# Two fill tiles and another order of the constant tiles in a one-layer hybrid encoder kernel

## The chip, the core and the metric

One NeuronCore of a Trainium2 chip runs the whole layer. The metric is the device time of one execution in microseconds (us); lower is better. The engines are called PE (TensorE, the matrix multiplier; PEld is its loading of stationary operands), DVE (VectorE), ACT (ScalarE), POOL (GpSimd) and SP (SyncE, which here only issues DMAs). SBUF is the on-chip memory from which PE reads both operands; each of its 128 partitions holds the same byte addresses, and "offset" below always means a tile's start address in a partition modulo 256 bytes.

## The reference

One encoder layer on x (1024 positions x 1024 features, float32):

```
h = rmsnorm(x);  p = h @ w_in                        (1024 x 3104)
yA = gb * dwconv3(gc * gv)                            gated short convolution
yB = silu(go) * headnorm(GLA_forward + GLA_backward)  gated linear attention, 4 heads, chunks of 64
x = x + rmsnorm(concat(yA, yB) @ w_out)
h = rmsnorm(x)
x = x + rmsnorm((silu(dwconv3(h @ w_up)_gate) * dwconv3(h @ w_up)_value) @ w_down)   D_FF = 2816
```

## The kernel before

Each large product is computed as three PE passes. An operand is split into a high part `h` (rounded to the fp32r format by an ACT copy, L687) and a low part `l` (the remainder, by a DVE subtraction, L688); then h x h, h x l and l x h are accumulated in PSUM. One PE instruction of these passes streams a moving operand of 128 partitions x 512 elements (2048 bytes per partition) through a stationary operand of 128 x 128 (512 bytes per partition), which a load instruction on PEld brings in first. In the trace's tile names the moving operand stands first behind the arrow and the stationary one second: `pa<-b1h,ug7h` streams b1h through ug7h into pa.

The stages, in order of time:

- The value projection (L345, streams of 272 elements) and the other input projections with the linear attention between them (`feature_chunk`, L232; L215 to L217 for the last one). The moving operands are hT (pool actp), the stationary ones weight pieces (pool wpool).
- `w_out_tile` (L734): eight row blocks of the output projection, 48 matmuls each. The moving operands are pieces of w_out, which lie where room is (pools mp, w2p, cvp); the stationary ones are the mixer's outputs yh, yl (actp). Between the blocks stand transposes (L762). At the end of the stage DVE makes the operands T1 to T5 of the next one.
- The up projection (`up(c)`, 22 units, L804). Each unit makes seven products of 12 matmuls, by a fast scheme that replaces eight block products by seven. The moving operands are b1, T1, T2 (actp) and T3, T4, T5 (pool act2, allocated from the right end of SBUF, behind pool mp's place). The stationary ones are weight pieces from `w_tile`, which takes six of every ten from wpool and four from w2p. While a unit runs, SP loads the next unit's weights, ACT and DVE split them, and DVE also adds the products into place and computes the convolutions (L961 to L963) and the gate (L1041, L1044).
- The down projection (`big_product`, `passes`, L1110): seven products over eleven pairs of feed-forward chunks. For each pair `operands(m, q)` loads both operands from HBM (SP, L1083 to L1088) and splits them; both parts of both operands lie in one tile of actp or act2, or (product 2, its first four pairs) in `w_tile` pieces.
- A last normalisation and the stores.

The POOL queue runs a side stream (`side`, `up_begin` to `down_end`, L93 to L130): it loads pieces of w_up and w_down, makes sums that the two fast schemes need, and stores them to HBM (tensors wud and wdd), from where SP loads them later. From unit 3 of the up projection on, each unit's first DVE addition (L988) releases an ACT copy `pace` (L991), for which one such job waits (two at units 8, 11 and 14). Three more jobs follow behind the up projection without a pace.

Where tiles lie: pools are placed one behind the other in the order in which they are opened. From the left: four small constants (to byte 1152), then cpool (ident, eps, prm), actp, ypool, wpool, rawp, `small`, and then the pools of the stages (gp, later w2p, cvp, sp and others). From the right end downwards: mp, later act2. A tile takes its size rounded up to 32 bytes. In cpool, ident (512 bytes, an identity matrix for transposes), eps (4) and prm (596) are allocated at L150, L152 and L276.

Of the kernel before, what the change touches and what calls it, by code (L numbers as in the profile page):

```python
# [8 lines left out]
F32 = mybir.dt.float32  # L9
# [7 lines left out]
P = 128  # L17
# [24 lines left out]
def kernel(  # L42
# [25 lines left out]
    w_up = w_up[0].rearrange("(k p) n -> p k n", p=P)  # L68
    w_down = w_down[0]

    cpool = ctx.enter_context(tc.tile_pool(name="cpool", bufs=1))
    actp = ctx.enter_context(tc.tile_pool(name="actp", bufs=4))
    ypool = ctx.enter_context(tc.tile_pool(name="ypool", bufs=8))
# [65 lines left out]
    def side(tile=row_tile, after=None, ahead=0):  # L139
# [5 lines left out]
        while len(begun) > ahead:  # L145
            end, i, t = begun.pop(0)
            with tc.issue_after(loads[-1].ins) if ahead else ExitStack():
                end(i, *t)

    ident = cpool.tile([P, P], F32, tag="ident", name="ident")  # L150
    make_identity(nc, ident)
    eps = cpool.tile([P, 1], F32, tag="eps", name="eps")  # L152
    nc.vector.memset(eps, EPS)
    small = ctx.enter_context(tc.tile_pool(name="small", bufs=4))

    pinned = [False]

# [45 lines left out]
    def act_table(name):  # L203
        tc.keep_in_program_order(nc.scalar.preload_act_table_set(name))
# [67 lines left out]
        yT[4 + h] = ypool.tile([P, L], F32, tag="y", name=f"yT{4 + h}")  # L272
        nc.scalar.activation(yT[4 + h], ps, AF.Silu)

    NPB = 21
    prm = cpool.tile([P, P + NPB], F32, tag="prm", name="prm")  # L276
    act_table("natural_log_exp_and_others")
    with ExitStack() as n1:
        np_ = n1.enter_context(tc.tile_pool(name="np", bufs=2))
# [131 lines left out]
        nc.tensor.transpose(pp[:, 0:P], stk[:, 0, :], ident)  # L411
        nc.tensor.transpose(pp[:, P : P + NPB], stk[0:NPB, 1, :], ident[0:NPB, 0:NPB])
        nc.vector.tensor_copy(prm, pp[:, 0 : P + NPB])

# [233 lines left out]
    def conv_steps():  # L648
        for j in range(4):
            yield from conv_tile(j, j == 3)  # L650
            yield

    fill = conv_steps()
# [582 lines left out]
```

## Time and profile before

| | |
|---|---|
| median of 3 runs | 1075.53 us (1074.16 to 1076.70) |
| the profiled execution | 1075.13 us, of which the span of its instructions is 1073.2 us |
| PE busy | 1057.0 us (98% of the span) |
| DVE busy | 801.8 us (75%) |
| ACT, POOL busy | 466.0 us (43%), 345.2 us (32%) |
| granted PE clock, mean | 0.999 of full |
| mean DMA rate | 196 GB/s |

A busy share sums an engine's instructions. PE's instructions overlap each other, so a PE that is busy all the time can still run faster or slower: its rate is the distance between the starts of two matmuls, which is read here from the chain of waits (the work that ended last, followed back from the end, with the stretch that each piece took). In the rows `xN` is a number of instructions, and L734 is line 734 of the program.

### The profile page before, as it was taken

The numbers are of one execution on the slowest core, as the hardware profiler recorded it, in microseconds if no ns is written. First come the engines' busy times: TensorE is split into PE (matmuls) and PEld (weight loads), VectorE is DVE, ScalarE is ACT, GpSimd is POOL, SyncE is SP. The second block draws the span as 40 slices with busy tenths as digits, with TensorE's granted clock in tenths as the row PEclk, the third lists the DMA queues.
The fourth block names the chain that finished last, engine by engine and source line by source line (L and its number), as shares of the span: only waits on it lengthen the run. The fifth ranks groups of instructions, "written<-read, shape, count | busy, mean of one in ns | idle before, by whom it ended". The sixth has DMA issues, their size and how long they took to land.

```text
span 1073.2 us, 14378 instructions
## 1 busy us (share of the span) xinstructions
PE 1057.0 (98%) x5409; PEld 871.0 (81%) x5409; DVE 801.8 (75%) x992; ACT 466.0 (43%) x654; POOL 345.2 (32%) x360
## 2 busy tenths in 40 slices
PE   8999999999999999999999999999999999999997
PEld 7998887888888888888888888888888777888886
DVE  6951369879867557988977988978998967556566
ACT  6431354463435234554344344343443435254452
POOL 2789500000000000004565564555546546400000
PEclk9999999999999999999999999999999999999999
DMA  8787511110255222167777877766976788976755
GB/s 287 271 273 257 177 41 40 40 40 21 72 164 168 79 79 95 44 195 245 258 239 244 280 251 229 249 211 180 298 262 223 264 323 294 351 244 229 243 176 216
DMA packets 163511, 210.64 MB, mean 196 GB/s; under 512 B 18273, under 2 KB 113650, under 8 KB 163442
## 3 DMA queue, kind: packets, MB, share of 16 engines
q1 hardware_dynamic: 142578, 134.48, 39.5%
q0 software_dynamic: 20288, 73.41, 19.5%
q10 hardware_dynamic: 576, 1.84, 0.4%
q8 instruction: 42, 0.69, 0.3%
q14 instruction: 27, 0.22, 0.1%
HBM read 146.52 MB, written 63.18 MB: 195 GB/s over the span
## 4 chain that ended last, share of the span: by engine, by line
PE 83%; DVE 8%; DMA 3%; ACT 2%; issue 2%; SPq 0%; DVEq 0%; ACTq 0%
PE pb L804 17%; PE pc L804 11%; PE pa L804 9%; PE pw L734 8%; PE pdb L1110 8%; PE pgc L232 4%; PE pgo L232 4%; PE pv L345 4%; PE pgv L232 3%; PE pqk L232 3%; PE pdd L1110 3%; PE pdc L1110 3%; PE pgb L232 2%; DVE d L688 1%; PE pdl L1110 1%
## 5 line engine op out<-in xcount | busy, mean ns | idle before, releaser
L100 POOL COPY wu10g<-pace 128x1 f32<-128x1 f32 x1 | 0.4, 354 | 365.7 <-ACT pace L991 365.7
L1110 PE MATMUL pdb<-d 128*128 128x512 f32 (+1 forms) x495 | 110.8, 384 | 0.4 <-DVE d L688 0.3
L1110 PEld LDWEIGHTS pdb<-d 128*128 128x128 f32 x495 | 90.5, 188 | 20.3 <-DVE d L688 1.6
L804 PE MATMUL pb<-t,uv 128*128 128x512 f32 x264 | 65.2, 396 | 0.0
L804 PEld LDWEIGHTS pb<-t,uv 128*128 128x128 f32 x264 | 49.6, 188 | 11.9
L988 DVE TENSOR_TENSOR cg<-cv,pb 128x512 f32<-128x512 f32 x22 | 15.1, 686 | 36.8 <-PE pb L804 16.6
L1041 ACT ACTIVATE uu<-uu 128x1024 f32<-128x1024 f32 x22 | 23.4, 1062 | 35.2 <-DVE uu L963 35.1
L1161 POOL DMA_DIRECT2D x2r<-x2d x4 | 2.1, 536 | 107.8 <-DMA d_8r<-actd 98.2
L1044 DVE TENSOR_TENSOR uu<-uu,uv 128x1024 f32<-128x1024 f32 x22 | 32.4, 1475 | 0.0
L962 DVE SCALAR_TENSOR_TENSOR uu<-cg,prm,uu 128x1023 f32<-128x1023 f32 x22 | 29.0, 1316 | 1.9
L1110 PE MATMUL pdc<-d 128*128 128x512 f32 x132 | 30.2, 390 | 0.0
L1110 PE MATMUL pdd<-d 128*128 128x512 f32 x132 | 30.2, 390 | 0.0
L963 DVE SCALAR_TENSOR_TENSOR uv<-cv,prm,uv 128x1023 f32<-128x1023 f32 x22 | 29.6, 1343 | 0.0
L873 ACT COPY cv<-pa 128x512 f32<-128x512 f32 x22 | 12.8, 587 | 38.1 <-PE pa L804 36.1
L963 DVE SCALAR_TENSOR_TENSOR uu<-cg,prm,uu 128x1023 f32<-128x1023 f32 x22 | 29.3, 1333 | 0.0
L1110 PEld LDWEIGHTS pdd<-d 128*128 128x128 f32 x132 | 24.8, 188 | 5.3
L1110 PEld LDWEIGHTS pdc<-d 128*128 128x128 f32 x132 | 24.8, 188 | 5.3
L962 DVE SCALAR_TENSOR_TENSOR uv<-cv,prm,uv 128x1023 f32<-128x1023 f32 x22 | 28.7, 1302 | 0.0
L570 DVE SCALAR_TENSOR_TENSOR S<-S,dec 64x128 f32<-64x128 f32 x56 | 19.2, 344 | 10.7 <-ACT S L561 8.5
L961 ACT ACTIVATE uv<-cv,prm 128x1024 f32<-128x1024 f32 x22 | 25.4, 1154 | 3.7 <-DVE cv L1021 3.5
L961 ACT ACTIVATE uu<-cg,prm 128x1024 f32<-128x1024 f32 x22 | 25.3, 1149 | 0.3 <-ACT d L687 0.3
L1018 DVE TENSOR_TENSOR cg<-cg,pc 128x512 f32<-128x512 f32 x22 | 15.0, 680 | 8.9 <-PE pc L804 8.9
(1314 smaller groups left out, 3252.3 us busy)
## 6 DMA issues: line engine op xcount, KB each, us to landing
actd<-as SPq DMA_DIRECT2D x20, 512.0 KB
x<-in_x_dram SPq DMA_DIRECT2D x16, 512.0 KB, 5.7
actd<-uu SPq DMA_DIRECT2D x10, 512.0 KB, 3.8
x2d<-x SPq DMA_DIRECT2D x8, 512.0 KB, 3.1
actd<-uu SPq DMA_DIRECT2D x10, 256.0 KB, 3.7
x2r<-x2d POOLq DMA_DIRECT2D x4, 512.0 KB, 5.5
x2r<-x2d SPq DMA_DIRECT2D x4, 512.0 KB, 4.5
out_dram<-o POOLq DMA_DIRECT2D x4, 512.0 KB, 7.1
```

The source lines that it names most:

```text
L232: nc.tensor.matmul(o[hf], wt[:, k, :], act[hf][a][:, k, :], start=(k == 0 and wt is wh and a == 0), stop=(k == KT - 1 and wt is wl))
L345: keep(nc.tensor.matmul(ps[:, n * 512 : n * 512 + VH], a[:, k, sl], w[:, k % 2, n * VH : (n + 1) * VH], start=(j == 0), stop=(j == 3 * KT ...
L570: nc.vector.scalar_tensor_tensor(S[0:DK, c + 1, :], S[0:DK, c, :], dec[0:DK, c : c + 1], S[0:DK, c + 1, :], op0=ALU.mult, op1=ALU.add)
L734: ins = nc.tensor.matmul(ps[:, n * HALF : (n + 1) * HALF], a[:, k, sl], w[:, n * HALF : (n + 1) * HALF], start=(i == 0 and q == 0), stop=( ...
L804: nc.tensor.matmul(o, w[:, k, :], m[:, k, :], start=start and k == 0 and q == 0, stop=k == 3 and q == 2, skip_group_check=True)
L961: nc.scalar.activation(u, src, AF.Copy, scale=ffn_tap(1, r))
L962: nc.vector.scalar_tensor_tensor(u[:, 1:L], src[:, 0 : L - 1], ffn_tap(0, r), u[:, 1:L], op0=ALU.mult, op1=ALU.add)
L963: nc.vector.scalar_tensor_tensor(u[:, 0 : L - 1], src[:, 1:L], ffn_tap(2, r), u[:, 0 : L - 1], op0=ALU.mult, op1=ALU.add)
L988: nc.vector.tensor_add(cg[:, hi], cv[:, lo], pb)
L1041: last_act[0] = nc.scalar.activation(ug, ug, AF.Silu)
L1044: nc.vector.tensor_mul(ug, ug, uv)
L1110: nc.tensor.matmul(o, a[:, 0, sl], b[:, 1, r], start=start and i == 0, stop=stop and i == 2, skip_group_check=True)
```

## The change

```diff
+    edge = ctx.enter_context(tc.tile_pool(name="edge", bufs=1, side="right"))
+    edge.tile([P, 56], F32, tag="fill", name="fill_r")
     cpool = ctx.enter_context(tc.tile_pool(name="cpool", bufs=1))
...
+    NPB = 21
+    eps = cpool.tile([P, 1], F32, tag="eps", name="eps")
+    prm = cpool.tile([P, P + NPB], F32, tag="prm", name="prm")
     ident = cpool.tile([P, P], F32, tag="ident", name="ident")
     make_identity(nc, ident)
-    eps = cpool.tile([P, 1], F32, tag="eps", name="eps")
     nc.vector.memset(eps, EPS)
     small = ctx.enter_context(tc.tile_pool(name="small", bufs=4))
+    small.tile([P, 48], F32, tag="fill", name="fill_l", bufs=1)
...
-    NPB = 21
-    prm = cpool.tile([P, P + NPB], F32, tag="prm", name="prm")
```

A fill of 224 bytes stands at the right end of SBUF, ahead of mp and act2; another of 192 bytes stands in `small`, ahead of all that follows it from the left; and ident comes behind eps and prm. No instruction reads or writes the fills. On every engine the same instructions stand in the same order as before, with the same waits; only addresses differ. Offsets (start address modulo 256) before and after, from the addresses in the built programs:

| tiles | bytes from the partition's start, before | offset before | after |
|---|---|---|---|
| actp, ypool, wpool, rawp (hT, yh, b1, T1, T2, most weight pieces, part of the down operands) | 2304 to 139776 | 0 | 0 |
| ident | 1152 | 128 | 0 |
| gp, w2p, cvp, sp (four of ten weight pieces, part of w_out, raw loads) | 142144 to about 180000 | 64 | 0 |
| mp, act2 (most of w_out, T3, T4, T5, part of the down operands) | 180192 to 229344 | 224 | 0 |

In unit 7 of the up projection the pieces ug7 and us7 lie in wpool and uv7 in w2p; its products follow each other as b1 x ug7, T2 x us7, b1 x ug7, T3 x us7, T1 x us7, T4 x uv7, T5 x us7 (moving x stationary).

The 128x512 matmuls by the offsets of their operands (moving / stationary) in the program before; after the change all of them are 0 / 0:

| line | 0/0 | 224/224, 64/64 | 224/0 | 0/64 | 224/64 | 64/0 | sum |
|---|---|---|---|---|---|---|---|
| L232, L215 to L217 | 960 | | | | | | 960 |
| L734 | | | 288 | | | 96 | 384 |
| L804 | 652 | | 472 | 404 | 320 | | 1848 |
| L1110 | 490 | 385 | | 8 | | 8 | 891 |

(L488 has eight more at 64/64.) The value projection's streams of 272 elements start at 0, 64, 128 and 192 before and after, since its halves are 1088 bytes long.

## Rows read from the trace of the kernel before

**Rows 1.** Page, part 1 and 2: busy us, share, instructions; granted clock in 40 slices.
```profile
PE   1057.0 (98%) x5409; PEld 871.0 (81%) x5409; DVE 801.8 (75%) x992; ACT 466.0 (43%) x654; POOL 345.2 (32%) x360
PEclk9999999999999999999999999999999999999999
```

**Rows 2.** Busy us (instructions) by stretch, then granted clock, DMA share, GB/s.
```profile
325.00:420.00 95.00, 95.00 (x437) 77.65 (x436) 55.81 (x101) 35.99 (x76) 0.00 (x0) 1.00 0.30 103
420.00:442.00 22.00, 21.89 (x104) 17.65 (x103) 21.89 (x40) 15.86 (x31) 0.00 (x0) 1.00 0.23 73
442.00:837.00 395.00, 395.00 (x1704) 319.78 (x1704) 341.54 (x342) 167.58 (x206) 195.26 (x193) 1.00 0.73 235
837.00:912.00 75.00, 73.08 (x313) 58.03 (x312) 56.80 (x45) 34.39 (x39) 43.03 (x41) 1.00 0.82 289
912.00:1073.20 161.20, 153.75 (x704) 127.61 (x704) 99.02 (x131) 68.95 (x104) 16.36 (x20) 0.99 0.71 243
```

**Rows 3.** PE lines: duration of one, ns min/median/max; first and last start.
```profile
L232 PE MATMUL pgo<-hTh,go2h x16: 389/389/389, 89.3 to 99.0; 128*128 128x512 f32 x16
...
L734 PE MATMUL pw<-wo6h,yl x16: 395/396/396, 329.3 to 411.9; 128*128 128x512 f32 x16
...
L1110 PE MATMUL pdc<-d x132: 387/389/398, 914.9 to 944.7; 128*128 128x512 f32 x132
```

**Rows 4.** Chain of waits: start us, us that the piece took, engine, output, line, matmuls.
```profile
313.96 0.87 PE pot L618 x8
...
325.74 55.73 PE pw L734 x240
381.47 1.75 PE tx L762 x16
```

**Rows 5.** The same chain: unit 7 of the up projection, and a product of the down projection.
```profile
558.84 2.76 PE pa L804 x12
561.60 2.72 PE pb L804 x12
564.32 2.72 PE pa L804 x12
567.04 2.80 PE pb L804 x12
569.84 2.74 PE pc L804 x12
572.59 2.81 PE pb L804 x12
575.40 2.80 PE pc L804 x12
...
945.12 30.09 PE pdb L1110 x132
```

**Rows 6.** The same chain between the up and the down projection.
```profile
837.10 0.70 DVE cg L988
...
857.94 6.45 DMA d_7r<-in_w_down_dram
...
874.18 11.35 DMA d_2r<-in_w_down_dram
...
892.28 8.61 DMA d_0r<-in_w_down_dram
...
903.98 4.84 DMA d_6r<-in_w_down_dram
...
912.23 2.80 PE pdb L1110 x11
```

**Rows 7.** POOL in order of time: start, us, instruction; in brackets what it waited for.
```profile
584.88 0.94 POOL L100 COPY wu15g<-pace 128x1 f32<-128x1 f32 x1 [2.28 <-ACT pace L991]
...
663.34 0.31 POOL L100 COPY wu19v<-pace 128x1 f32<-128x1 f32 x1 [2.81 <-DMA wud<-wu18g]
```

**Rows 8.** DVE groups in 130 to 190 us: count, busy us, mean ns, idle before.
```profile
L511 DVE TENSOR_TENSOR qd<-qd,m 128x1024 f32<-128x1024 f32 x2 | 2.5, 1225 | 1.6 <-ACT m L507 1.6
...
L191 DVE TENSOR_TENSOR qk2l<-qk2r,qk2h 128x1024 fp32r<-128x1024 f32 x1 | 1.2, 1224 | 3.2 <-ACT qk2h L190 3.2
```

## The prediction

> **What bounds the kernel now.** I read the page's busy shares first: PE has 98% of the span, DVE 75%, and the granted clock is at its full level, 2.4 GHz, in every slice [rows 1]. So only two things can bring time: PE's few waits, or the distance between its matmuls. The stretches say where each counts [rows 2]. From 325 to 420 (output projection) and from 442 to 837 us (up projection) PE is busy for the whole of the stretch and every other engine less; there the stage lasts as long as its matmuls stand apart. From 420 to 442 DVE is busy for 21.89 of 22.00 us: it makes T1 to T5, and a faster PE gains nothing. From 837 to 912 PE is busy for 73.08 of 75, yet the chain of waits does not run over it: it runs through DVE, the issue of operand loads and the loads themselves, 6.45, 11.35, 8.61 and 4.84 us of them [rows 6]. PE is nearly filled there, but its end is set by loads.
>
> Then the distances. The chain gives the time of whole products. In unit 7 of the up projection, seven products of 12 matmuls, one after the other on a PE that waits for nothing, take 2.76, 2.72, 2.72, 2.80, 2.74, 2.81 and 2.80 us [rows 5]. The four short ones are those whose operands both start at offset 0 (b1 and T2 or T1 with wpool pieces); the three long ones pair 224 with 0 or with 64. Short: 10.94 us / 48 = 227.9 ns per matmul. Long: 8.41 / 36 = 233.6 ns. The difference, 5.7 ns, stands inside one stage and one unit, beside the same DVE, POOL and DMA work. The output projection, where every moving operand starts at 224 or 64 and every stationary one at 0, takes 55.73 us / 240 = 232.2 ns [rows 4]. A product of the down projection, whose two operands mostly lie in one tile (0/0 or 224/224), takes 30.09 / 132 = 228.0 ns [rows 5]. So a tile at 224 is not slow in itself; two operands at different offsets are. The durations of single matmuls say the same: 389 ns in the input projections at 0/0 and in the down projection, 395 to 396 in the output projection [rows 3].
>
> **The change part by part.** It adds no instruction and takes none away; order and waits on every engine, SP's and POOL's queues among them, stay as they are. It moves addresses, and after it every 128x512 matmul is 0/0.
>
> - Output projection: 384 matmuls. (232.2 - 228.0) x 384 = 1.6 us. Its end starts the DVE work of 420 to 442, which keeps its length but starts earlier, so all 1.6 us pass through.
> - Up projection, 442 to 837: 395.00 us / 1704 = 231.8 ns now [rows 2]; at 227.9 the stretch is 3.9 x 1704 = 6.6 us shorter. (The other way: 1196 of 1848 matmuls have unequal offsets, x 5.7 ns = 6.8 us for all 22 units.) It passes through if DVE keeps up: 341.54 us of work against 395.00 now and 388.4 then, 88% busy. I count it whole.
> - 837 to 912: the chain of loads begins at DVE's addition at 837.10, right behind a product of PE, so it starts earlier by what came before and keeps its 75.1 us [rows 6]. PE's own gain here, some 70 pairs, I cost at nothing: the loads cover it.
> - Behind 912: nearly all pairs are equal already; the borders between actp and act2 tiles and the sixteen 0/64 and 64/0 matmuls are some 40 pairs x 6 ns = 0.2 us.
> - Input projections: all 0/0 already, nothing. Streams of 128: eight transposes with operands at 128 and 224 take 0.87 us and sixteen at 128 and 0 take 1.75 [rows 4], 109 ns each both times, so moving ident and the small operands costs or brings nothing.
> - DVE: a subtraction with all operands at 0 takes 1224 ns and a product with all at 224 takes 1225 [rows 8]; nothing.
> - The fills are never touched: nothing.
>
> Sum: 1.6 + 6.6 + 0.2 = 8.4 us. Against the profiled execution, 1075.13 - 8.4 = 1066.7; the median shown, 1075.53, lies 0.4 higher, so **1067.1 us**. What the trace doesn't show is how near an all-equal stage comes to its best product. Bounds: every matmul as in the shortest products, 2.72 / 12 = 226.7 ns, gives (231.8 - 226.7) x 1704 = 8.7, (232.2 - 226.7) x 384 = 2.1 and 1.3 x 528 = 0.7 in the down projection, together 11.5 us (1064.0); the other end is no gain. I take 227.9 to 228.0, because it is what equal pairs reach on average beside the same traffic, in two stages.
>
> Against the change speaks the Trainium skill, "TensorE: Matmul & The Clock Gate", sections "Back-to-back issue gap" and "Step-by-step: what each phase is for": the gap depends on the number of columns and the clock alone, and loading the next weights doesn't take read bandwidth from the running matmul. By it the sum would be 0 and the time 1075.5. The trace disagrees so far: 227.9 and 233.6 ns for the same columns at the same clock [rows 5].
>
> **The rivals.**
>
> *Offsets are not the cause.* What the slow products share could also be that one operand lies in the upper part of SBUF (above 142144 bytes) and the other in the lower. Then nothing changes: 1075.5 us. For it: 224/224 pairs lie in one tile and are fast. Against it: T4 with uv7 lie both in the upper part, at 224 and 64, and that product is the longest of the unit, 2.81 us [rows 5]. Chance 0.09.
>
> *Part is given back to the side stream.* From unit 8 on POOL's jobs no longer wait for `pace` (a job at 584.88 still does) but for their own stores (one at 663.34) [rows 7], so POOL runs at its own rate. By 585 PE has gained 1.6 + 6.6 x 143 / 395 = 4.0 us, by 837 8.2: POOL lags by 4.2 us more against PE, and its loads and stores then share the 16 DMA engines with the operand loads, which decide from 837 on. If those lose what POOL lags, 4.2 us go back: 1071.3. Against it: only the share of the loads that meets POOL's moves. It shows as longer waits of PE for d. Chance 0.17.
>
> *Slower.* The same place, one step worse. Of the four loads on the chain two took 11.35 and 8.61 us and two 6.45 and 4.84 [rows 6]. If PE's earlier arrival lets POOL's bursts meet the two short ones as well, at 11.35 each, that is 4.9 + 6.5 = 11.4 us more, against 8.4 gained: 1075.5 + 3.0 = 1078.5. It turns into a loss from 8.4 us of longer loads. Against it: POOL's traffic doesn't grow, and what it does later leaves room earlier. Chance 0.05.
>
> **How the numbers follow.** Forecast 0.69, the rivals 0.09, 0.17 and 0.05. A measurement of this kernel tells about 0.2%, 2.2 us, from no change. Forecast and partial give-back lie below 1073.4: 0.86, less 0.02 for a give-back that takes nearly all, 0.84 faster; same 0.11; slower 0.05. The range goes from the best-product bound, 1064.0, to 1072.0, just past the give-back, and leaves out the other two rivals and the tails, together under 0.2.
>
> **What would show it.** Right: unit 7's seven products all at 2.72 to 2.76 us; the 240-matmul piece of the output projection near 54.7 us in place of 55.73; 442 to 837 shrunk to some 388 us for the same matmuls; the 30.09 us products of the down projection unchanged; the stretch from the last up products to PE's piece at 912 still about 75 us. Wrong: products still at 2.80, which means the first rival; or products at 2.73 and that stretch grown by several us with PE waiting for d, which means the second or the third. A granted clock below full in any stage but the last would upset the sum too.

## The result, and the profile after

The changed kernel takes 1065.25 us, median of 4 runs (1063.65 to 1065.81), against 1075.07 us for the kernel before, median of 4 (1074.16 to 1076.70). The ratio is 0.9905, with a 95% interval of 0.9887 to 0.9922: 9.8 us faster. The forecast was 1067.1, in a range of 1064.0 to 1072.0. The profiled execution of the changed kernel took 1065.09 us, its span 1063.1 us, 10.1 less than before.

The diff adds lines near the top and takes two out further down, so most of the program stands four lines lower: L804 is now L808, L734 is L738, L1110 is L1114, L687 and L688 are L691 and L692, and so on.

The page of the changed kernel, which answers to [rows 1]:

```profile
PE 1045.8 (98%) x5409; PEld 871.3 (82%) x5409; DVE 800.1 (75%) x992; ACT 466.3 (44%) x654; POOL 344.0 (32%) x360
PEclk9999999999999999999999999999999999999999
```

There is the same number of instructions on every engine, and the granted clock is the same. PE's busy time fell by 11.2 us at an unchanged share.

The stretches, asked for at the same times as [rows 2] (busy us and instructions of PE, PEld, DVE, ACT, POOL; clock; DMA share; GB/s):

```profile
420.00:442.00 22.00, 21.84 (x104) 17.57 (x103) 21.98 (x40) 15.91 (x30) 0.00 (x0) 1.00 0.19 63
442.00:837.00 395.00, 394.56 (x1739) 325.76 (x1738) 348.00 (x346) 172.52 (x210) 199.45 (x197) 1.00 0.73 240
837.00:912.00 75.00, 71.97 (x313) 58.04 (x312) 53.57 (x42) 31.06 (x35) 45.38 (x42) 1.00 0.89 311
```

In 395 us PE now gets through 1739 matmuls, where it was 1704. DVE is busy for 348.00 of the 395 and just keeps up.

PE's groups by line (duration of one in ns, min/median/max; first and last start). The T4 and T5 products with uv, before the change:

```profile
L804 PE MATMUL pb<-t,uv x264: 391/396/400, 453.3 to 847.7; 128*128 128x512 f32 x132
```

The changed kernel; the second and third row answer to [rows 3]:

```profile
L808 PE MATMUL pb<-t,uv x264: 387/389/398, 450.8 to 837.6; 128*128 128x512 f32 x132
L738 PE MATMUL pw<-wo6h,yl x16: 389/389/389, 329.0 to 409.9; 128*128 128x512 f32 x16
L1114 PE MATMUL pdc<-d x132: 389/389/389, 904.9 to 934.5; 128*128 128x512 f32 x132
L1114 PE MATMUL pdl<-d x66: 279/336/389, 1024.5 to 1054.8; 128*128 128x512 f32 x33, 128*128 128x256 f32 x33
```

The first and last starts tell where the time went. The first matmul of T4 and T5 with uv starts 2.5 us earlier, the last one 10.1 us earlier. The down projection's pdc product, behind the stretch that loads decide, starts 10.0 us earlier (914.9 in [rows 3]). The last matmul starts 10.9 us earlier (1065.7 before).

The chain of waits, in the output projection and in unit 7 of the up projection; its pieces answer to [rows 4] and [rows 5]:

```profile
325.55 54.40 PE pw L738 x240
379.95 1.75 PE tx L766 x16
...
553.90 2.72 PE pa L808 x12
556.62 2.72 PE pb L808 x12
559.34 2.72 PE pa L808 x12
562.06 2.72 PE pb L808 x12
564.78 2.72 PE pc L808 x12
567.50 2.72 PE pb L808 x12
570.22 2.72 PE pc L808 x12
```

All seven products of the unit take 2.72 us, 226.7 ns per matmul. The 240 matmuls of the output projection take 54.40 us, also 226.7 ns each. Products of 128 columns are unchanged (1.75 for sixteen).

Behind the up projection the chain now stays with the loads and with ACT and DVE, which split what was loaded, to the end. Some of its pieces, which answer to [rows 6]:

```profile
827.23 0.70 DVE cg L992
...
848.14 5.95 DMA d_7r<-in_w_down_dram
...
865.75 10.73 DMA d_3r<-in_w_down_dram
...
906.21 5.41 DMA d_5r<-in_w_down_dram
...
923.96 7.06 DMA d_0r<-wdd
```

PE nevertheless hardly waits there; these are its waits of more than 0.3 us behind 442 us (which instruction waited for which: us in total, times, longest):

```profile
PE pdb L1114 <- DVE d L692: 1.2, 1, 1.2
PE pda L1114 <- DVE d_2l L692: 1.0, 1, 1.0
PE pda L1114 <- DVE d_3l L692: 0.7, 1, 0.7
PE pc L808 <- DVE cv L1011: 0.4, 1, 0.4
```

Loads and PE end their work almost together: the chain changed its owner, and PE lost 3.3 us in all, against 2.0 before.

### The profile page after: what moved, and what is told of

The parts are those of the page before. It is cut to its first block, busy times and chain, and to the rows that moved or that the text cites. A ratio compares the mean times of both kernels' runs of the same rounds, so it can differ in the third digit from the quotient of the medians.

```text
span 1063.1 us, 14378 instructions
## 1 busy us (share of the span) xinstructions
PE 1045.8 (98%) x5409; PEld 871.3 (82%) x5409; DVE 800.1 (75%) x992; ACT 466.3 (44%) x654; POOL 344.0 (32%) x360
## 4 chain that ended last, share of the span: by engine, by line
PE 68%; DVE 14%; DMA 10%; ACT 4%; issue 4%; SPq 1%; DVEq 0%; ACTq 0%
PE pb L808 16%; PE pc L808 11%; PE pa L808 9%; PE pw L738 8%; PE pgc L238 4%; PE pgo L238 4%; DVE d L692 4%; PE pv L349 4%; PE pgv L238 3%; PE pqk L238 3%; PE pgb L238 2%; DMA d_3r<-in_w_down_dram 1%; ACT d L691 1%; DMA d_7r<-wdd 1%; DMA d_9r<-in_w_down_dram 1%
## 5 line engine op out<-in xcount | busy, mean ns | idle before, releaser
L1114 PE MATMUL pdb<-d 128*128 128x512 f32 (+1 forms) x495 | 109.8, 383 | 1.2 <-DVE d L692 1.2
L1114 PEld LDWEIGHTS pdb<-d 128*128 128x128 f32 x495 | 90.7, 188 | 20.0 <-DVE d L692 2.0
L808 PE MATMUL pb<-t,uv 128*128 128x512 f32 x264 | 63.5, 389 | 0.0
L808 PEld LDWEIGHTS pb<-t,uv 128*128 128x128 f32 x264 | 49.6, 188 | 10.3
L1114 PE MATMUL pdc<-d 128*128 128x512 f32 x132 | 30.1, 389 | 0.0
L1114 PE MATMUL pdd<-d 128*128 128x512 f32 x132 | 30.1, 389 | 0.0
L1114 PEld LDWEIGHTS pdc<-d 128*128 128x128 f32 x132 | 24.8, 188 | 5.2
L1114 PEld LDWEIGHTS pdd<-d 128*128 128x128 f32 x132 | 24.8, 188 | 5.1
L574 DVE SCALAR_TENSOR_TENSOR S<-S,dec 64x128 f32<-64x128 f32 x56 | 19.2, 344 | 10.7 <-ACT S L565 8.5
L578 DVE SCALAR_TENSOR_TENSOR S<-S,dec 64x128 f32<-64x128 f32 x56 | 19.7, 352 | 1.9
```

Source lines behind the costliest of these rows:

```text
L578: nc.vector.scalar_tensor_tensor(S[DK:P, c - 1, :], S[DK:P, c, :], dec[DK:P, c : c + 1], S[DK:P, c - 1, :], op0=ALU.mult, op1=ALU.add)
L808: nc.tensor.matmul(o, w[:, k, :], m[:, k, :], start=start and k == 0 and q == 0, stop=k == 3 and q == 2, skip_group_check=True)
L1114: nc.tensor.matmul(o, a[:, 0, sl], b[:, 1, r], start=start and i == 0, stop=stop and i == 2, skip_group_check=True)
```

## The experiments

The theory "relation" says that a 128x512 matmul is slow when its two operands' offsets differ, wherever they lie, and that a few equal ones behind it are slow as well. Its rival "absolute" says that starting at a multiple of 256 is what counts. The prediction's second rival (POOL falls behind PE, and its transfers lengthen the operand loads) is taken up last. Kernels e1 to e4 ran beside each other, against a before of 1075.9 us (median of 23 runs); so did the repeat and e5, against 1076.0 us (17 runs). The microseconds gained are worked out from the ratios. The scan is one execution of each kernel.

### One fill without the other

e1, the right end back at 224:

```diff
-    edge = ctx.enter_context(tc.tile_pool(name="edge", bufs=1, side="right"))
-    edge.tile([P, 56], F32, tag="fill", name="fill_r")
```

> The fill at the right end of SBUF is left out, so mp and act2 (most of w_out, T3, T4, T5, part of the down operands) start at 224 again; everything from the left is at 0. Pairs of 128x512 matmuls: 2630 at 0/0, 1080 at 224/0, 381 at 224/224. Theory 'relation' (a matmul is slow when its two operands' offsets differ, and the next few equal ones behind it are slow as well): before had 1596 unequal pairs and the whole change brought 9.8 us; 1080 are left, so 9.8 x 516 / 1596 = 3.2 us gained, 1071.9 us. Unit 7: T3, T4 and T5 products at about 2.80, the product right behind one of them 2.74 to 2.76, the others 2.72. The w_out piece of 240 matmuls about 55.7. Theory 'absolute' (each operand off a multiple of 256 costs by itself, and the cost adds): the down products with 224/224 operands were no slower before, so it has to say that only the stationary operand at 64 counts, or only the moving one at 224: then the gains of this kernel and of the one with only the other fill sum to 9.8.

Measured: 1073.19 us, ratio 0.9969 (0.9953 to 0.9985), so 3.3 us gained. Unit 7 in its chain:

```profile
557.93 2.75 PE pa L806 x12
560.68 2.72 PE pb L806 x12
563.40 2.72 PE pa L806 x12
566.12 2.80 PE pb L806 x12
568.92 2.75 PE pc L806 x12
571.66 2.80 PE pb L806 x12
574.47 2.80 PE pc L806 x12
```

As "relation" expected: T3, T4 and T5 at 2.80, the two equal products right behind an unequal one at 2.75, the two others at 2.72. T4 x uv7, with uv7 now at 0 and T4 still at 224, is no faster for that.

e2, gp, w2p and cvp back at 64:

```diff
-    small.tile([P, 48], F32, tag="fill", name="fill_l", bufs=1)
```

> The fill in the pool small is left out, so gp, w2p and cvp (four of ten weight pieces, part of w_out) start at 64 again; the right end is at 0. Pairs: 3243 at 0/0, 732 at 0/64, 104 at 64/0, 12 at 64/64. Theory 'relation': 836 of 1596 unequal pairs are left, 9.8 x 760 / 1596 = 4.7 us gained, 1070.4 us; together with the other half (3.2) only 7.9 of 9.8, because 320 pairs (224/64) were unequal by both. Unit 7: only T4 with uv7 at about 2.80, the product behind it 2.74 to 2.76, the five others 2.72. The w_out piece of 240 near 54.7. Theory 'absolute': the two halves sum to 9.8, that is 6.6 us here, 1068.6, if the other half gains 3.2.

Measured: 1072.13 us, ratio 0.9971 (0.9955 to 0.9987), 3.1 us gained; expected were 4.7, at the edge of the interval. From its chain, the piece of the output projection, and in unit 7 T1 x us7, T4 x uv7 and T5 x us7:

```profile
325.74 54.97 PE pw L737 x240
...
567.77 2.72 PE pc L807 x12
570.49 2.80 PE pb L807 x12
573.29 2.75 PE pc L807 x12
```

The products are as expected; the output projection is not (54.97 for "near 54.7"). Only 60 of its 240 matmuls are unequal here (64/0), and they cost 0.57 us above 54.40, 9.5 ns each. In the scan below, 180 such matmuls in longer runs cost 0.72 us, 4 ns each. In e2 they stand in groups of 2 and 6 between equal ones. Worked out from the starts, they are 233.5 ns apart there, against 229.5 in the scan, and the six equal ones behind a group of six are slow as well, at 231.5. So the cost of a pair hangs on what stands ahead of it too, and gains need not follow the count of unequal pairs. The totals are too wide to show that: the two halves brought 6.4 us together, with about 1.7 us to either side of each, where the count of pairs expected 7.9. "Absolute" wanted 9.8 of that sum; what decides on it is the next run.

### All operands off the multiple, all alike

e3:

```diff
-    edge.tile([P, 56], F32, tag="fill", name="fill_r")
+    edge.tile([P, 40], F32, tag="fill", name="fill_r")
...
+    cpool.tile([P, 16], F32, tag="fill", name="fill_c")
     ident = cpool.tile([P, P], F32, tag="ident", name="ident")
```

> The changed kernel with 64 bytes more ahead of ident and the right fill 64 bytes smaller, so that all 4091 pairs are 64/64: no operand starts at a multiple of 256, and no pair is unequal. Theory 'relation': as the changed kernel, 1065.3 us, products of the up projection at 2.72. Theory 'absolute' (the start at a multiple of 256 is what counts): every pair costs what the unequal ones did before, 5.7 ns or more x 4091 = 23 us, 1088 us, products at 2.80.

Measured: 1067.92 us (1067.28 to 1069.72, 6 runs), ratio 0.9924 (0.9902 to 0.9947). Three pieces of its chain, the output projection, T4 x uv7 and a product of the down projection:

```profile
325.82 54.40 PE pw L739 x240
...
568.09 2.72 PE pb L809 x12
...
908.64 29.92 PE pdc L1115 x132
```

The first two are to the hundredth as in the changed kernel, with every operand at 64. "Absolute" wanted 1088 and 2.80 and has fallen. The total of 1065.3 was missed, and not by scatter: all six runs lie above the nine of the changed kernel (1063.65 to 1066.16, the repeat below included). The 2.6 us do not come from the products. In the profile one down product had to wait 2.5 us for an operand. And SP's 62 transfers issued from 442 to 820 us took, worked out from the trace, a median of 4.56 us from issue to landing, against 3.80 and 3.85 in the two profiles of the changed kernel; from 820 to 905 us, where that wait arose, no such difference is seen (6.00 against 5.62 and 6.37). What makes the 2.6 us stays open.

### ident alone

e4, ident first in its pool again, at 128:

```diff
+    ident = cpool.tile([P, P], F32, tag="ident", name="ident")
     eps = cpool.tile([P, 1], F32, tag="eps", name="eps")
     prm = cpool.tile([P, P + NPB], F32, tag="prm", name="prm")
-    ident = cpool.tile([P, P], F32, tag="ident", name="ident")
```

> The changed kernel with ident first in its pool again (at 128 in place of 0); all 128x512 pairs stay at 0/0. The part of the change that moves ident is undone alone. Both theories, and the prediction: nothing, 1065.3 us, since eight transposes took 0.87 us in both kernels and ident stands in no 512-wide matmul. If transposes do care for the offset, some 100 of 109 ns each by at most 6 ns, 0.6 us.

Measured: 1066.11 us, ratio 0.9909 (0.9889 to 0.9929), the same as the whole change within the intervals. The order of the constants brings nothing; the two fills are the change.

### Which differences cost: a scan

The right fill was made 48, 40, 32, 24, 16 or 8 elements long, so that mp and act2 lie at 32 to 192 and all else at 0. In the output projection 180 of the 240 matmuls then pair that offset with 0, and T3, T4 and T5 do in unit 7.

> The changed kernel with the right fill 32 bytes smaller: mp and act2 start at 32, all else at 0; 1080 pairs at 32/0, 381 at 32/32, 2630 at 0/0. Measured by the w_out piece of 240 matmuls (moving operand from mp, stationary at 0) and by unit 7's T3, T4, T5 products. Theory 'relation to 256': unequal, so like 224/0: the piece about 55.7 us, the products 2.80. Rival 'smaller unit': if only a difference off a multiple of 32 counts, as after, 54.4 and 2.72.

> As the one before with mp and act2 at 64: 1080 pairs at 64/0. Relation to 256: the piece about 55.0 (64/0 pairs stood about 229 ns apart in the kernel before, 0/64 about 233), products 2.75 to 2.80. Unit of 64 bytes: 54.4 and 2.72.

> The changed kernel with mp and act2 at 96: 1080 pairs at 96/0, the one multiple of 32 not seen yet. No row shows its price; 32/0, 128/0, 192/0 and 224/0 stood 233.3 to 233.5 ns apart and 64/0 229. Expected as the four: the w_out piece of 240 about 55.7 us, products 2.80. If the price falls towards a difference of 64: 55.0 to 55.4 and 2.76 to 2.78.

> As the one before with mp and act2 at 128: 1080 pairs at 128/0. Relation to 256: slower than 54.4 and 2.72, by how much no row shows; 55.7 and 2.80 if every unequal pair costs the same. Unit of 128 bytes: 54.4 and 2.72.

> The changed kernel with mp and act2 at 160: 1080 pairs at 160/0. The same difference modulo 256 as the 224/64 pairs of the kernel before, whose gaps went round in a cycle of seven (231 234 235 233 232 238 237 ns, mean 233.7 to 234.3). Theory 'relation to 256, by the difference alone': the same cycle here, though neither offset is the same; the w_out piece of 240 about 56.1 us, products 2.81. If the absolute offsets count: another cycle, as the 224/0 pairs (235 and 232 in turn).

> As the one before with mp and act2 at 192: 1080 pairs at 192/0, the moving operand 64 bytes short of the stationary one's offset, as in the 0/64 pairs of the kernel before (233 ns). Relation to 256, by the difference alone: 55.9 and 2.80, that is slower than 64/0. If the sign of the difference does not count, 192/0 and 64/0 cost the same.

Measured (0 is the changed kernel, 224 is e1; the last column is the mean distance from the start of an unequal 128x512 matmul to the next start, over the whole trace, gaps of more than 300 ns left out):

| moving minus stationary | output projection x240, us | T4 x uv7, us | whole kernel, us | unequal pairs, ns |
|---|---|---|---|---|
| 0 | 54.40 | 2.72 | 1065.25 | 227.0 (all) |
| 32 | 55.77 | 2.80 | 1075.50 | 233.4 |
| 64 | 55.12 | 2.76 | 1069.48 | 229.8 |
| 96 | 55.90 | 2.81 | 1076.97 | 234.0 |
| 128 | 55.76 | 2.79 | 1071.14 | 232.8 |
| 160 | 55.99 | 2.81 | 1073.62 | 234.0 |
| 192 | 55.60 | 2.80 | 1073.13 | 233.3 |
| 224 | 55.74 | 2.80 | 1073.19 | 233.5 |

No unit smaller than 256 bytes is enough: 32, 64 and 128 all cost. A multiple of 256 is enough, as the changed kernel shows: by the addresses of its program 2092 of the matmuls counted have operands an even multiple of 256 bytes apart and 1938 an odd one, and they stand at 227.06 and 226.95 ns. Six of the seven differences cost the same within 1.2 ns, and +64 costs half. The sign counts: +64 stands at 229.8, -64 (192) at 233.3. The totals rank nothing, since the twelve runs of e1 alone spread from 1071.35 to 1076.96 us.

The rhythm within a product is the strictest test. Distances from start to start in ns, worked out from the starts in the trace:

```
before, T4 x uv7,  224/64:  231 237 238 231 234 235 233 232 237 238 231 231
160/0,  T3 x us7,  160/0:   235 231 231 232 237 238 231 234 235 234 231 237
160/0,  unit 6, T4-T5:      235 233 232 238 237 231 234 235 233 232 238 237
e1,     T3 x us7,  224/0:   234 235 232 235 232 235 231 235 232 235 232 235
e1,     T1 behind T3, 0/0:  230 235 229 232 231 227 226 227 227 226 227 227
after,  behind transposes:  229 233 236 224 231 236 228 233 230 227 227 226
```

160/0 goes round in the cycle of seven that 224/64 had (231 234 235 233 232 238 237), not in that of 224/0, though it shares neither offset with 224/64. Here the difference alone fixes the cycle. That isn't so everywhere: 0/64 in the kernel before alternates between 231 and 236, 192/0 between 233 and 234, at the same mean. And the mean hangs on the neighbours too: 64/0 stands at 229.8 here and in the kernel before, and at 233.4 in e2, where it comes in short groups between equal pairs. The last two rows show the settling: an equal stream needs several matmuls to come down to 226.7, five behind 224/0 and nine behind these transposes. It is not a fixed number: behind 160/0 it takes three, and behind two other groups of transposes in the changed kernel two.

### The second rival: a late POOL

The changed kernel again, unaltered, and e5, where copies into the fill delay POOL's queue:

```diff
+            for j in range(40 if c == 12 else 0):
+                nc.gpsimd.tensor_copy(fill_r[:, j : j + 1], pace)
             for _ in range(2 if c in (8, 11, 14) else 1):
                 side(late_tile, pace)
```

> The changed kernel once more, unaltered, beside the same runs of before as the kernel with the late POOL: 1065 to 1066 us. Its profile shows how much PE's waits behind 800 us scatter from run to run: they were 3.3 us in the first profile of it (1.2, 1.0, 0.7 and 0.4), and 4.5 to 5.5 in the two kernels whose products are as fast (all at 64, and ident at 128). If the scatter is as large within this kernel, the difference between these three is no property of theirs.

> The changed kernel with forty copies of one number (0.18 us each in the rows of this engine) put into POOL's queue ahead of the job wu21, into the fill at the right end, which nobody reads: the side stream is some 7 to 8 us later against PE from about 690 us on. The second rival of the prediction priced a lag of POOL of 4.2 us at up to 4.2 us of longer operand loads: by it 7 to 8 us go back, 1073. The theory 'covered' (POOL's jobs are needed late, and the loads have slack that PE does not see): less than 2 us go back, 1065 to 1067.

The repeat: 1065.32 us, ratio 0.9900 (0.9882 to 0.9917). e5: 1067.57 us (1064.27 to 1081.32, 12 runs), ratio 0.9931 (0.9906 to 0.9955). e5 decides nothing, since its lag against the repeat did not last. The copies took 5.82 us, and the job behind them, wu21g, began at 696.41 against 690.60. But the repeat's own POOL then fell behind that of the first profile, and 63 us later the two stood 1.9 us apart (759.86 against 757.98), as they had ahead of the copies (the store of wu19g at 672.74 against 670.89). And e5's profiled run was already 1.6 us behind the repeat's at 45 us, so its total isn't read as a price.

One POOL store, the second behind `down_end`, in the timelines of three kernels: before, then the first profile of the changed kernel, then the repeat (start, us, instruction):

```profile
758.36 0.58 POOL L130 DMA_DIRECT2D wdd<-wd1r  x1 [0.42 <-POOL wd1r L128]
```

```profile
748.25 0.58 POOL L133 DMA_DIRECT2D wdd<-wd1r  x1 [0.42 <-POOL wd1r L131]
```

```profile
757.98 0.58 POOL L133 DMA_DIRECT2D wdd<-wd1r  x1 [0.42 <-POOL wd1r L131]
```

In the first profile POOL came along with PE, 10.1 us earlier than before. In the repeat the same program's POOL was 9.7 us later, about where before had it. That lag was gone when the loads began to decide. The store of wd11r, ten stores on, in the same three timelines:

```profile
851.07 0.57 POOL L130 DMA_DIRECT2D wdd<-wd11r  x1 [0.41 <-POOL wd11r L128]
```

```profile
841.27 0.57 POOL L133 DMA_DIRECT2D wdd<-wd11r  x1 [0.41 <-POOL wd11r L131]
```

```profile
841.85 0.57 POOL L133 DMA_DIRECT2D wdd<-wd11r  x1 [0.41 <-POOL wd11r L131]
```

Here POOL is 9.8 and 9.2 us earlier than before, as much as DVE's addition at the head of the chain of loads (837.10 before, 827.23 and 827.91 after). PE's rows of the repeat:

```profile
L1114 PE MATMUL pdc<-d x132: 388/389/390, 904.9 to 934.5; 128*128 128x512 f32 x132
L1114 PE MATMUL pdl<-d x66: 279/336/390, 1024.5 to 1055.5; 128*128 128x512 f32 x33, 128*128 128x256 f32 x33
```

The product pdc starts at 904.9 in both, and PE's waits behind 442 us are 3.9 us in the repeat and 3.3 in the first profile (5.5 in e3, 5.2 in e4). So a lag of 9.7 us at 750 us that is gone by 841 costs nothing that can be told. The stretch that the rival prices is 837 to 912. POOL's 40 instructions of it start 6.8 to 10.3 us earlier than before in the first profile and 8.9 to 10.2 in the repeat, PE's last up products and pdc 9 to 10 us: nowhere is POOL 4.2 us behind. What such a lag would cost there no run shows.

## Why the prediction was right, and where its size was off

**The cause.** Right: two operands at different offsets, not one at 224 or 64. The reading of unit 7, three long products out of seven, came out in full: all seven are at 2.72, and e3 shows that alike is enough. The rival "offsets are not the cause" has fallen with it: the fills moved the upper tiles by at most 224 bytes, left them in the upper part, and the cost went. The Trainium skill ("TensorE: Matmul & The Clock Gate", "Back-to-back issue gap") gives the gap by the columns and the clock and names no offsets. The scan disagrees: 227.0 to 234.0 ns at 512 columns and the full clock, by the offsets. Which resource the two operands share, no run here shows.

**Output projection.** 1.6 us predicted. PE began 0.2 earlier at 325 us, which nothing in the change explains, and the up projection's first whole product on the chain, pa, 2.2 us earlier (442.54 before, 440.30 after): 2.0 between them. DVE's stretch of 420 to 442 passed it through, as predicted.

**Up projection.** 6.6 predicted; from 2.2 to 10.1 us earlier is 7.9. DVE kept up but for 0.4 us (1.2 in the repeat).

**837 to 912.** Nothing predicted, since loads decide. From DVE's addition (837.10 before, 827.23 after) to the first pdc matmul (914.9 and 904.9) it was 77.8 us and is 77.7. Right.

**Down projection.** 0.2 predicted; from 10.0 to 10.9 is 0.9. That its 30.09 us products would not change was wrong: in e3, whose chain shows them, they take 29.92 us. In the changed kernel too, from the first start of one to that of the next, and four of them make 0.7 us of the 0.9.

**The end.** Not in the prediction: 0.8 us of it is lost behind the last matmul, which was 7.5 us from the end of the span and is 8.3. Over all profiles of this document it lies between 7.5 and 8.7, so this is scatter.

The sum is 0.2 + 2.0 + 7.9 - 0.1 + 0.9 - 0.8 = 10.1 us of the profiled run; 8.4 had been predicted. **The term that was mis-sized** is the short distance itself: "Short: 10.94 us / 48 = 227.9 ns per matmul", and the 228.0 of the down projection. That mean is over two kinds. The products of 2.76 and 2.74 in [rows 5] stand right behind an unequal one and were still settling; the two of 2.72 had an equal one ahead of them. e1 repeats the pattern, and in the changed kernel no unequal pair is left to settle from: over its whole trace its pairs stand 227.0 ns apart (gaps of more than 300 ns left out), where the equal pairs of the kernel before stood at 228.05. The maximum of 398 beside a median of 389 in the down projection [rows 3] was the same trace of it, and became 389/389/389. The prediction had 226.7 as its far bound and chose against it, on the ground that equal pairs beside the same traffic averaged 228. The traffic was not what slowed them. With 226.7 its sum was 11.5 us; the last matmul came 10.9 us earlier.

**The other rivals.** The give-back to POOL failed at its premise: in the stretch that it prices, POOL came along with PE in both profiles and was nowhere 4.2 us behind. Its price stays untested. The slower case, two more loads at 11.35 us, did not come: of the six load pieces that the chain has up to 912 us one took 10.73 us and the others 3.55 to 8.17. In both profiles of the changed kernel loads, ACT and DVE own the chain behind the up projection, so that a still faster PE should gain little there; no run tried it.

## What to carry to other kernels

When one matmul shape shows two distances in one stage, sort the products by the start addresses of both operands modulo 256 bytes, and place the pools so that the two agree; two small fills can be enough. To the matmuls the common offset made no difference here (0 and 64), but the kernel with all at 64 was 2.6 us slower for a reason that stays open. Take as the price of a good product the shortest one with another good one ahead of it, not the mean, and count changes between kinds as well as pairs. After a gain on the bounding engine, look at what ends the chain: here it went to the operand loads within 10 us of it.

## What the runs showed of the hardware that was not expected

- A stream of equal-offset 128x512 matmuls settles at 226.7 ns (12 in 2.72 us, 132 in 29.92); unequal ones go round in cycles of distances, with means in the scan of 229.8 (+64) and 232.8 to 234.0 ns (the other differences).
- Behind unequal pairs and behind 128-column transposes the next equal matmuls are slow, up to nine of them, 224 to 236 ns each. Products right behind an unequal one lost 0.03 us by it in e1 (2.75 for 2.72).
- +64 costs half of -64 in the scan (229.8 and 233.3 ns), and as much as the others in short groups between equal pairs (233.4 in e2). Why, and why 0/64 and 192/0 have different cycles at one price, no run here tells.
- POOL's side stream takes different phases in two runs of one program: 9.7 us apart at one store at 750 us, 0.6 us apart at another at 841 us, with no effect on the time that can be told.
